# Modulation matmuls with 32 columns a quadrant, one copy out of the bank, and the first weights loaded ahead of x

## The chip, the cores and the metric

The kernel runs on one core of a Trainium2 chip. The metric is device time in microseconds (us) of one execution, as the median of several runs. The engines are named TensorE (PE in the rows; its weight loads are PEld), VectorE (DVE), ScalarE (ACT), GpSimd (POOL) and SyncE (SP), the last of which issues most of the DMA transfers.

## The reference, cut to what matters

Two layers of a hybrid backbone, fp32 throughout, for 128 context tokens and 1024 latent tokens of 1024 features. Every layer scales and shifts its normalised input by a modulation that is computed from a condition vector:

```
def ada_modulate(x, cond, norm_g, w_ada, b_ada):
    m = jax.nn.silu(cond) @ w_ada + b_ada
    shift, scale, gate = jnp.split(m, 3, axis=-1)
    h = rms_norm(x, norm_g) * (1.0 + scale[:, None, :]) + shift[:, None, :]
    return h, gate[:, None, :]
```

There are two condition vectors, `c` for the latent tokens and `c_ctx` for the context tokens, so this product has two rows; `w_ada` is 1024 x 3072 for each layer. Layer 0 then projects h by `w_in_0`, runs a convolution module and an attention side by side, and projects out; layer 1 does the same with a pooling mixer. In both, `x + gate * out` is returned.

## The kernel before, in words

Tokens go in 9 tiles of 128 (tile 8 is the context), three tiles to a group g of 384 columns. Features are cut into 8 chunks k of 128. A product in fp32 precision is made of three fp32r matmuls, of high and low parts: `split` casts a weight to its high part on ScalarE (L186) and subtracts it on VectorE for the low part (L187).

The modulation product puts the two condition vectors, after silu, as the stationary operand. `sc` (L144) holds 8 chunks x 2 columns; a matmul loads the 2 columns of a chunk and streams a strip of `w_ada`. Four strips run side by side, one in each column group of the array (`tile_position=(0, r)`, r = 0, 32, 64, 96), and so fill rows r and r + 1 of a PSUM bank. The program's fp32 matmuls appear in the trace as two records each.

Shift and scale of layer 0 come in four rounds m. `load_wada(m)` (L288) issues four strips of 512 KB on SP and, from round 1 on, one small vector behind each (`late`); `ada0_rows(m)` (L319) has the 32 matmuls and copies the four row pairs out to `ads` by four VectorE copies (L333); `ada0_cols(m)` (L335) turns them by one transpose (L338) and adds bias and norm gain into `SH` and `SC` (L273, L278, L279), two chunks k a round. All that layer 1 needs, and the gates, comes later in three strip sets, `ada_strips` (L350), 8 steps of four matmuls each, given out as background work by `ada_steps`; `ada_cols` (L379) clears a tile on GpSimd (L383) and copies four row pairs (L385), and `ada_turn` transposes it.

The start: SP issues four small vectors (one of them on ScalarE's queue), x0 to x2, the strips of round 0, the first halves of two weights (`raw0`), x3 to x5, rounds 1 and 2, the second halves, round 3, x6 and x7. `norm_x` squares a tile on ScalarE (L126), makes the reciprocal root on GpSimd (L113, L114) and scales on VectorE (L128). `h_chunk` (L441) transposes a chunk of three x tiles (L445), applies SC and SH on ScalarE (L450) and splits the result (L451, L452). `first_chains` (L470) writes by hand, under `manual_schedule`, the order of TensorE, ScalarE and VectorE: round m, then its h chunks, and the chain matmuls (L230) that they allow. `split_w0(0, 0)`, the split of the first half weight, stands ahead of that block in the program. Elsewhere a planner orders each engine's instructions by a simulated timeline. Behind `first_chains` come the rest of the projections with the convolution as background work on VectorE, ScalarE and GpSimd, the attention, the output product and layer 1.

Of the kernel before, what the change touches and what calls it, by code (L numbers as in the profile page):

```python
# [10 lines left out]
F32 = mybir.dt.float32  # L11
F32R = mybir.dt.float32r
AF = mybir.ActivationFunctionType
ALU = mybir.AluOpType
AX = mybir.AxisListType
P = 128
EPS = 1e-6
NEG = -1e30
D = 1024
# [27 lines left out]
def _body(tc, nc, A, O, const, wp, arena, tmpp, smp, psp):  # L47
# [7 lines left out]
    def slot(i, dtype=F32, name="s"):  # L55
        return arena.tile([P, SLOT], dtype, tag=f"S{i}", bufs=1, name=nm(name))
# [22 lines left out]

    ident = const.tile([P, P], F32, name="ident")  # L80
    make_identity(nc, ident)
    mhalf = const.tile([P, 16], F32, name="mhalf")
    gp.memset(mhalf, -0.5)
    corr = {}
    for w in (2, 4, 8, 16):
# [21 lines left out]
    def load_x(t):  # L107
        xt[t] = slot(XS[t], name="x")[:, :D]
        last["x"] = sy.dma_start(xt[t], x_src(t)).ins
# [9 lines left out]
    def norm_x(t):  # L119
        if t in normal:  # L120
            return
        normal.add(t)
        if t not in xt:
            load_x(t)
        ss = small(1, "ss")
        se.activation(gr[:, :D], xt[t], AF.Square, accum_out=ss)  # L126
        r = rstd_of(ss, D, 1.0 / D)
        ve.tensor_scalar(xt[t], xt[t], r, None, ALU.mult)  # L128

    last = {}  # L130
    for t in range(3):
        load_x(t)

    NV, NV0 = 102, 48
    V = const.tile([P, NV], F32, name="V")
# [5 lines left out]
    se.activation(th0, V[:, :16], AF.Tanh, scale=0.5)  # L141
    cu = small(16, "cu")
    ve.scalar_tensor_tensor(cu, th0, 1.0, V[:, :16], ALU.add, ALU.mult)
    sc = const.tile([P, 8, 2], F32, name="sc")  # L144
    ve.tensor_scalar(sc.rearrange("p k c -> p c k"), cu.rearrange("p (c k) -> p c k", c=2), 0.5, None, ALU.mult)

    vq = const.tile([P, 12], F32, name="vq")
    qn8, lgh, lbh = vq[:, 0:1], vq[:, 1:5], vq[:, 5:9]
# [3 lines left out]
    rows2, cwn = tmp("rows2"), tmp("cwn")  # L152
    knb = const.tile([P, 64], F32, name="knb")

    late = [
        (rows2[r0 - NV0 : r0 - NV0 + n, :P], src.rearrange("(r p) -> r p", p=P))
        for r0, src, n in (
            (V_CB, A["conv_b_0"], 4), (V_NG[1], A["norm_g_1"], 8), (V_BA[1], A["b_ada_1"], 24),
# [119 lines left out]
        ve.tensor_tensor(dst[:, k0 : k0 + n, :], src, b, ALU.add)  # L278
        ve.scalar_tensor_tensor(dst[:, k0 : k0 + n, :], dst[:, k0 : k0 + n, :], 1.0, g, ALU.add, ALU.mult)  # L279


    WAS = (0, 1, 4, 5, 2, 3, 6, 7, 8, 9, 10, 11, 16, 21, 22, 23)
    ads = [const.tile([P, P], F32, name=f"ads{i}") for i in range(2)]
    for t in ads:
        gp.memset(t, 0.0)
    for t in range(3):
        norm_x(t)
    first_w, wt = {}, {}  # L288

    def load_wada(m):  # L290
        for kh in range(2):
            for x in range(2):
                t = slot(WAS[4 * m + 2 * kh + x], name="wada")[:, :D].rearrange("p (k c) -> p k c", c=256)
                c0 = x * D + m * 256
                sy.dma_start(t, A["w_ada_0"][kh * 512 : (kh + 1) * 512, c0 : c0 + 256].rearrange("(k p) c -> p k c", p=P))
                wt[m, kh, x] = t
                if m and late:
                    sy.dma_start(*late.pop(0))

    raw0 = {}  # L300

    def split_w0(c, u):
        first_w[c, u] = split(*raw0[c, u])

    load_wada(0)
    raw0[0, 0] = load_raw0(0, 0)
    raw0[1, 0] = load_raw0(1, 0)
    for t in range(3, 6):
# [5 lines left out]
    load_wada(3)  # L314
    for t in (6, 7):
        load_x(t)
    split_w0(0, 0)
    adb = {}

    def ada0_rows(m):  # L320

        b = adb[m] = bank("tp")
        for k in range(8):
            for x in range(2):
                for q in range(2):
                    r = 32 * (2 * x + q)
                    te.matmul(
                        b[r : r + 2, :P], sc[:, k, :], wt[m, k // 4, x][:, k % 4, q * P : (q + 1) * P],
                        start=(k == 0), stop=(k == 7), tile_position=(0, r),
                    )  # L330
        t = ads[m % 2]
        for r in range(0, P, 32):
            ve.tensor_copy(t[r : r + 2, :], b[r : r + 2, :P])  # L333

    def ada0_cols(m):  # L335

        adt = adb[m][:, P : 2 * P]
        te.transpose(out=adt[:, :98], in_=ads[m % 2][:98, :], identity=ident[:98, :98])  # L338
        av = adt.rearrange("p (x q c) -> p x q c", x=2, q=2)
        fin_shift(0, SH[0], av[:, 0, :, 0:2], 2 * m, 2)  # L340
        fin_scale(0, SC[0], av[:, 1, :, 0:2], 2 * m, 2)
# [6 lines left out]
    def ada_strips(l, col, n, fin):  # L348

        st = {}  # L350

        def step(k):
            w = slot(ADS[st_i[0] % len(ADS)], name="wad")[:, : 4 * n]
            st_i[0] += 1
            dma_later(w, A[f"w_ada_{l}"][k * P : (k + 1) * P, col : col + 4 * n])
            if k == 0:
                st["b"] = bank("tp")
            for q in range(4):
                r = 32 * q
                te.matmul(  # L360
                    st["b"][r : r + 2, :n], sc[:, k, :], w[:, q * n : (q + 1) * n],
                    start=(k == 0), stop=(k == 7), tile_position=(0, r),
                )
            if k == 7:
                st["then"] = fin(st["b"])


        then, owed_turn[:] = list(owed_turn), [lambda: st["then"] and st["then"]()]
        adq.append(then + [lambda k=k: step(k) for k in range(4)])
        adq.append([lambda k=k: step(k) for k in range(4, 8)])  # L370
# [8 lines left out]
    def ada_cols(l, b, c0):  # L379

        t = slot(ADS[st_i[0] % len(ADS)], name="adr")[:, :G]
        st_i[0] += 1
        gp.memset(t[:98, :], 0.0)  # L383
        for r in range(0, P, 32):
            ve.tensor_copy(t[r : r + 2, :], b[r : r + 2, :G])  # L385
        return lambda: ada_turn(l, t, c0)

    def ada_turn(l, t, c0):
# [78 lines left out]
    def first_chains():  # L467


        bs = {(0, 0): (bank("mm"), bank("mm")), (1, 0): (bank("mm"), bank("mm")), (0, 1): (bank("cv"), bank("cv"))}  # L470

        def C(k, which=((0, 0), (1, 0), (0, 1))):
            for x, g in which:
                w = [first_w[x, 0], first_w.get((x, 1))]
                for i in range(2):
                    chain_ws(bs[x, g][i][:, :G], w, i * P, h0, g, ks=(k,))

        def T(k, g):
            h_chunk(g, [xt[t] for t in range(3 * g, 3 * g + 3)], 0, h0, k, "tp")

        h0[0] = hslots(range(4))
        ada0_rows(0)
        ada0_cols(0)
        T(0, 0)
        T(1, 0)
        for k in range(2):
            C(k, ((0, 0),))
        split_w0(1, 0)
        for t in range(3, 6):
            norm_x(t)  # L490
        h0[1] = hslots(range(4, 8))
        for k in range(2):
            C(k, ((1, 0),))
        T(0, 1)
        T(1, 1)
        ada0_rows(1)
        for k in range(2):
            C(k, ((0, 1),))
        ada0_cols(1)
        for k in (2, 3):  # L500
            for g in range(2):
                T(k, g)
        for m in (2, 3):
            ada0_rows(m)
            C(2 * m - 2)
            ada0_cols(m)
            T(2 * m, 0)
            T(2 * m, 1)
            if m == 2:
                split_w0(0, 1)  # L510
            C(2 * m - 1, ((0, 0), (1, 0)))
            T(2 * m + 1, 0)
            T(2 * m + 1, 1)
            if m == 2:
                split_w0(1, 1)
            C(2 * m - 1, ((0, 1),))
        for x in bs:
            for k in (6, 7):
                C(k, (x,))
        return bs  # L520
# [959 lines left out]
```

## Time and profile before

| | us |
|---|---|
| median of 3 runs (967.46 to 968.0) | 967.62 |
| the profiled execution | 967.13 |
| its span | 965.4 |
| TensorE matmul busy | 940.7 (97%) |
| VectorE busy | 602.5 (62%) |
| ScalarE busy | 403.8 (42%) |
| GpSimd busy | 368.7 (38%) |

Times in the rows below are microseconds from the span's start unless marked ns. A line of the timeline gives start, duration, engine, source line, operation, output and inputs, and in brackets the idle time of the engine ahead of it with what ended it; instructions of one kind in a row are merged (x4). A q behind an engine's name is its sequencer, which issues DMAs. The duration of a matmul holds its way through the array, so the pace of a stream is read from a merged piece in the chain of waits, divided by its count.

### The profile page before, as it was taken

The page shows a single profiled execution, that of the slowest core. Times are in us where ns is not written, and L with a number is a line of the kernel's source. Part 1 is how long each engine was busy: PE and PEld are TensorE (multiplying, and loading weights), DVE is VectorE, ACT ScalarE, POOL GpSimd, SP SyncE. Part 2 cuts the span into 40 slices and gives each one's busy share as a digit, 9 for nine tenths or more (in the row PEclk, how much of TensorE's full clock was granted, in tenths as well). Part 3 has the DMA queues.
Part 4 walks back from the last instruction along what each step waited for, and adds up shares of the span by engine and source line. Part 5 has one row for each costly group of instructions (what it writes and reads, how often), then busy time and mean ns, then how long its engine had stood idle before and what let it go on. Part 6 is the DMA issues. An engine that isn't in the chain of part 4 may idle for free.

```text
span 965.4 us, 16658 instructions
## 1 busy us (share of the span) xinstructions
PE 940.7 (97%) x6388; PEld 863.5 (89%) x6388; DVE 602.5 (62%) x1243; ACT 403.8 (42%) x815; POOL 368.7 (38%) x485
## 2 busy tenths in 40 slices
PE   4899999999999999999999999999999999999998
PEld 2799999899999999987777888899999999998887
DVE  3659999999683444457778547656335455585332
ACT  4365667675611344248886323353222222231010
POOL 2354879999944201124456246430000000004331
PEclk9999999999999999999999999999999999999999
DMA  9956955426111111135344413241110011133311
GB/s 310 301 202 142 352 197 185 154 67 230 48 47 48 47 45 44 43 100 144 116 122 149 151 44 119 98 145 44 55 41 30 30 44 55 66 117 124 109 66 66
DMA packets 87531, 108.53 MB, mean 112 GB/s; under 512 B 10701, under 2 KB 73037, under 8 KB 87340
## 3 DMA queue, kind: packets, MB, share of 16 engines
q1 hardware_dynamic: 82539, 95.93, 31.2%
q0 software_dynamic: 2576, 9.18, 2.4%
q10 hardware_dynamic: 2336, 2.36, 0.7%
q8 instruction: 50, 0.82, 0.4%
q14 instruction: 30, 0.24, 0.1%
HBM read 94.64 MB, written 21.57 MB: 120 GB/s over the span
## 4 chain that ended last, share of the span: by engine, by line
PE 81%; POOL 8%; DMA 5%; ACT 2%; DVE 2%; issue 1%; SPq 1%; DVEq 0%; ACTq 0%; POOLq 0%
PE mm L230 38%; PE mm L1216 10%; PE mm L1209 10%; PE mm L237 8%; POOL zc L555 7%; PE cv L987 3%; DMA wada<-in_w_ada 3%; PE tp L978 2%; PE mm L954 2%; PE mm L1379 2%; PE tp L445 1%; DMA raw<-in_w_in 1%; DMA raw<-in_w_out 1%; PE tp L360 1%; DMA wad<-in_w_ada 1%
## 5 line engine op out<-in xcount | busy, mean ns | idle before, releaser
L230 PE MATMUL mm<-h,whi 128*128 128x384 f32 x1504 | 388.0, 338 | 1.0 <-POOL h L452 0.4
L230 PEld LDWEIGHTS mm<-h,whi 128*128 128x128 f32 x1504 | 271.3, 188 | 4.4 <-issue 1.7
L230 PE MATMUL mm<-h,wlo 128*128 128x384 f32 x752 | 252.4, 336 | 0.0
L555 POOL TENSOR_TENSOR zc<-zc,gr 128x384 f32<-128x384 f32 x138 | 148.8, 1079 | 31.2 <-ACT gr L553 22.8
L237 PE MATMUL mm<-whi,h 128*128 128x256 f32 x864 | 156.8, 284 | 0.6 <-DVE qk L731 0.6
L230 PEld LDWEIGHTS mm<-h,wlo 128*128 128x128 f32 x752 | 141.6, 188 | 0.0
L237 PEld LDWEIGHTS mm<-whi,h 128*128 128x128 f32 x864 | 135.1, 192 | 2.7 <-issue 0.7
L237 PE MATMUL mm<-wlo,h 128*128 128x256 f32 x432 | 122.3, 283 | 0.0
L187 DVE TENSOR_TENSOR wlo<-raw,whi 128x1024 fp32r<-128x1024 f32 (+1 forms) x56 | 68.2, 1219 | 46.8 <-ACT whi L186 46.5
L566 DVE SCALAR_TENSOR_TENSOR cv<-u,convw,cv 128x384 f32<-128x384 f32 (+2 forms) x208 | 94.8, 511 | 0.8
L1216 PE MATMUL mm<-wrh,zs 128*128 128x512 f32 x288 | 92.3, 392 | 0.4 <-POOL wrh L1183 0.4
L1209 PE MATMUL mm<-whi,zs 128*128 128x512 f32 (+1 forms) x304 | 92.5, 379 | 0.0
L186 ACT CAST whi<-raw 128x1024 fp32r<-128x1024 f32 (+1 forms) x56 | 56.9, 1018 | 64.4 <-PE mm L230 25.4
L237 PEld LDWEIGHTS mm<-wlo,h 128*128 128x128 f32 x432 | 82.9, 192 | 0.0
L1223 POOL TENSOR_TENSOR y<-y,og 128x512 f32<-128x512 f32 x34 | 48.6, 1430 | 83.2 <-DVE og L1221 80.1
L553 ACT ACTIVATE gr<-u,convw 128x384 f32<-128x384 f32 (+2 forms) x128 | 64.5, 531 | 29.5 <-POOL zc L555 29.0
L972 POOL TENSOR_SCALAR p<-p,st 128x512 f32<-128x512 f32 x64 | 47.9, 760 | 46.5 <-DVE st L970 30.6
L1209 PEld LDWEIGHTS mm<-whi,zs 128*128 128x128 f32 x304 | 56.0, 188 | 10.6 <-ACT whi L186 0.2
L1216 PEld LDWEIGHTS mm<-wrh,zs 128*128 128x128 f32 x288 | 53.9, 188 | 12.0 <-POOL wrh L1183 0.8
L1221 DVE TENSOR_TENSOR og<-mm,gr 128x512 f32<-128x512 f32 x34 | 23.3, 687 | 59.3 <-PE mm L1216 34.3
L535 ACT ACTIVATE th<-mm 128x384 f32<-128x384 f32 x48 | 23.5, 489 | 81.7 <-PE mm L230 81.6
L1209 PE MATMUL mm<-wlo,zs 128*128 128x512 f32 (+1 forms) x152 | 57.2, 378 | 0.0
(215 smaller groups left out, 1393.3 us busy)
## 6 DMA issues: line engine op xcount, KB each, us to landing
raw<-in_w_in SPq DMA_DIRECT2D x28, 512.0 KB
wad<-in_w_ada SPq DMA_DIRECT2D x16, 768.0 KB
wada<-in_w_ada SPq DMA_DIRECT2D x16, 512.0 KB
raw<-in_w_in SPq DMA_DIRECT2D x32, 256.0 KB
raw<-in_w_out SPq DMA_DIRECT2D x16, 512.0 KB
y0scr<-y POOLq DMA_DIRECT2D x9, 512.0 KB, 3.1
y<-y0scr SPq DMA_DIRECT2D x9, 512.0 KB
x<-in_x_sample SPq DMA_DIRECT2D x8, 512.0 KB
```

The lines of the kernel that those rows point to most:

```text
L186: se.copy(hi[:, :n], raw[:, :n])
L187: ve.tensor_tensor(lo[:, :n], raw[:, :n], f(hi[:, :n]), ALU.subtract)
L230: te.matmul(out, wsl(units, a, k, c0, P), hsl(hs, b, k, g), start=(k == 0 and i == 0), stop=(k == nk - 1 and i == 2))
L237: te.matmul(out, hsl(hs, p, k, g, a, P), wsl(units, q, k, 0, 256), start=(k == 0 and i == 0), stop=(k == 7 and i == 2))
L553: se.activation(pr[:, o : o + n], src, AF.Copy, scale=w)
L555: gp.tensor_tensor(z, z, pr, ALU.add)
L566: ve.scalar_tensor_tensor(zp if k == 30 else acc, src, convw[:, c, k : k + 1], zp if k == NPTS[c] else acc, ALU.mult, ALU.add)
L972: gp.tensor_scalar(ps[i][:, e, :], ps[i][:, e, :], st[:, 4 + e : 5 + e], 0.0, ALU.mult, ALU.add)
L987: te.matmul(ob[64 * e : 64 * e + 64, i * P : (i + 1) * P], vw[j0 + i][x][:, 64 * e : 64 * e + 64], pts[i][:, e, n * P : (n + 1) * P], star ...
L1209: te.matmul(b[:, c0 : c0 + n], zs[p][:, k, :], WL[k // 2][q][:, k % 2, c0 : c0 + n], start=(k == 0 and i == 0), stop=(k == 7 and i == 2))
L1216: te.matmul(b, zs[p][:, k, :], WR[q][k // 3][:, k % 3, :], start=(k == 0 and i == 0), stop=(k == 7 and i == 2))
L1223: gp.tensor_tensor(yv, yv, t, ALU.add)
```

## The change

`sc` gets 48 columns, of which the last 32 are zero, and each modulation matmul loads 32 columns from column 2k on, so that it fills all 32 rows of its quadrant (rows 0 and 1 are the wanted ones, the others hold sums of other chunks' vectors with this strip, which nothing reads). One VectorE copy of all 128 partitions takes the place of four copies of 2, in the four rounds and in the later strips, and the memsets of `ads` and of the later tiles go. The strips of round 0 are issued ahead of x0 to x2; the normalisation of x0 to x2 moves behind the other loads in the program; and the split of the first half weight moves into the hand-written order, behind `ada0_cols(0)`.

```
-    mhalf = const.tile([P, 16], F32, name="mhalf")
+    mhalf = const.tile([P, 8], F32, name="mhalf")
...
     last = {}
-    for t in range(3):
-        load_x(t)
...
+    wt, late = {}, []
...
+    load_wada(0)
...
-    sc = const.tile([P, 8, 2], F32, name="sc")
-    ve.tensor_scalar(sc.rearrange("p k c -> p c k"), cu.rearrange("p (c k) -> p c k", c=2), 0.5, None, ALU.mult)
+    sc = const.tile([P, 48], F32, name="sc")
+    gp.memset(sc, 0.0)
+    ve.tensor_scalar(sc[:, :16].rearrange("p (k c) -> p c k", c=2), cu.rearrange("p (c k) -> p c k", c=2), 0.5, None, ALU.mult)
...
     ads = [const.tile([P, P], F32, name=f"ads{i}") for i in range(2)]
-    for t in ads:
-        gp.memset(t, 0.0)
-    for t in range(3):
-        norm_x(t)
...
-    load_wada(0)
+    for t in range(3):
+        load_x(t)
     raw0[0, 0] = load_raw0(0, 0)
...
     for t in (6, 7):
         load_x(t)
-    split_w0(0, 0)
+    for t in range(3):
+        norm_x(t)
...
-                        b[r : r + 2, :P], sc[:, k, :], wt[m, k // 4, x][:, k % 4, q * P : (q + 1) * P],
+                        b[r : r + 32, :P], sc[:, 2 * k : 2 * k + 32], wt[m, k // 4, x][:, k % 4, q * P : (q + 1) * P],
...
-        t = ads[m % 2]
-        for r in range(0, P, 32):
-            ve.tensor_copy(t[r : r + 2, :], b[r : r + 2, :P])
+        ve.tensor_copy(ads[m % 2], b[:, :P])
...
-                    st["b"][r : r + 2, :n], sc[:, k, :], w[:, q * n : (q + 1) * n],
+                    st["b"][r : r + 32, :n], sc[:, 2 * k : 2 * k + 32], w[:, q * n : (q + 1) * n],
...
-        gp.memset(t[:98, :], 0.0)
-        for r in range(0, P, 32):
-            ve.tensor_copy(t[r : r + 2, :], b[r : r + 2, :G])
+        ve.tensor_copy(t, b[:, :G])
...
         ada0_rows(0)
         ada0_cols(0)
+        split_w0(0, 0)
         T(0, 0)
```

## Rows read from the trace of the kernel before

**Rows 1.** The page: TensorE's busy time over the span, and two lines of the span in 40 equal slices of 24.1 us, in tenths.

```profile
PE 940.7 (97%) x6388; PEld 863.5 (89%) x6388; DVE 602.5 (62%) x1243; ACT 403.8 (42%) x815; POOL 368.7 (38%) x485
...
PE   4899999999999999999999999999999999999998
...
DMA  9956955426111111135344413241110011133311
```

**Rows 2.** Busy time of each engine by stage (the first three rows are of one table over the whole span, its first and last stage and its sum; the last is of a finer table of the start). Columns: stage, its length, busy time and count of PE, PEld, DVE, ACT, POOL, granted clock of TensorE, DMA share, GB/s.

```profile
0.00:50.00 50.00, 33.51 (x375) 26.68 (x376) 26.69 (x56) 19.76 (x30) 15.86 (x61) 1.00 0.98 303
...
870.00:965.40 95.40, 91.67 (x428) 76.69 (x426) 34.75 (x42) 9.87 (x17) 30.12 (x27) 1.00 0.25 88
sum 965.40, PE 940.75 PEld 863.46 DVE 602.46 ACT 403.81 POOL 368.70; mean PE 49.51 PEld 45.45 DVE 31.71 ACT 21.25 POOL 19.41
...
20.00:25.00 5.00, 4.29 (x15) 3.89 (x16) 3.60 (x5) 4.84 (x8) 3.04 (x5) 1.00 1.08 357
```

**Rows 3.** The chain of waits at the start, its three longest transfers: from issue, for so long.

```profile
18.25 8.04 DMA wada<-in_w_ada
...
26.31 7.50 DMA wada<-in_w_ada
...
37.49 10.17 DMA wada<-in_w_ada
```

**Rows 4.** The timeline around the fourth round: its last matmuls, its row copies, the transpose behind them.

```profile
47.71 1.04 PE L327 MATMUL tp<-wada,sc 128*2 128x128 f32 x28 [0.65 <-DMA wada<-in_w_ada]
...
48.84 1.18 DVE L333 COPY ads<-tp 2x128 f32<-2x128 f32 x4
...
51.93 0.25 PE L338 MATMUL tp<-ident,ads 98*128 98x98 f32 x1
```

**Rows 5.** The transfer view of the first 60 us: what the DMA engines moved in each 1.5 us.

```profile
GB/s 0 27 251 399 395 381 356 350 342 298 291 365 412 390 354 347 348 351 350 349 345 339 304 292 308 229 201 321 371 307 194 223 215 285 295 44 5 41 344 426
```

**Rows 6.** SP's queue: the first two issues of large transfers (timeline), and what it waited for up to 38.1 us (the longest and the shortest in total of the five waits for transfers: us in total, times, longest).

```profile
1.88 1.30 SPq L109 DMA_DIRECT2D x<-in_x_sample  x3
...
3.23 2.99 SPq L295 DMA_DIRECT2D wada<-in_w_ada  x4
...
SPq L295 <- DMA wada<-in_w_ada: 4.5, 4, 1.8
...
SPq L298 <- DMA raw<-in_w_in: 0.5, 1, 0.5
```

**Rows 7.** The timeline of the start: square and scaling of x2, the last quarter of round 0, the cast of the first half weight, the row copies, the low part, and the first chain matmul; then the same pair of matmuls at two times.

```profile
8.27 1.06 ACT L126 ACTIVATE gr<-x 128x1024 f32<-128x1024 f32 x1
...
10.61 0.76 DVE L128 TENSOR_SCALAR x<-x,rstd 128x1024 f32<-128x1024 f32 x1 [0.71 <-POOL rstd L114]
...
14.29 1.87 PE L327 MATMUL tp<-wada,sc 128*2 128x128 f32 x28 [0.95 <-DMA wada<-in_w_ada]
...
16.12 1.04 ACT L186 CAST whi<-raw 128x1024 fp32r<-128x1024 f32 x1 [6.71 <-DMA raw<-in_w_in]
16.21 1.19 DVE L333 COPY ads<-tp 2x128 f32<-2x128 f32 x4 [4.84 <-PE tp L327]
...
17.43 1.22 DVE L187 TENSOR_TENSOR wlo<-raw,whi 128x1024 fp32r<-128x1024 f32 x1
...
20.32 0.69 PE L230 MATMUL mm<-h,whi 128*128 128x384 f32 x1 [0.39 <-DVE h L451]
...
22.21 0.84 PE L230 MATMUL mm<-h,whi 128*128 128x384 f32 x2
...
24.09 0.51 PE L230 MATMUL mm<-h,whi 128*128 128x384 f32 x2
```

**Rows 8.** Single lines of the program: the row copies of the rounds and of the later strips, the memset that goes (duration in ns as min/median/max, first and last start), and one other copy out of PSUM (timeline).

```profile
L333 DVE COPY ads<-tp x16: 271/286/297, 16.2 to 49.7; 2x128 f32<-2x128 f32 x16
...
L385 DVE COPY adr<-tp x8: 539/553/567, 160.0 to 198.0; 2x384 f32<-2x384 f32 x8
...
L383 POOL MEMSET adr<- x2: 425/425/425, 139.1 to 179.4; 98x384 f32 x2
...
3.53 0.21 DVE L138 COPY V<-tp 128x48 f32<-128x48 f32 x1 [3.53 <-PE tp L137]
```

**Rows 9.** TensorE's wait behind 75 us that comes from VectorE (timeline), and two pieces of the chain of waits that leads to it.

```profile
236.54 0.36 PE L237 MATMUL mm<-whi,h 128*128 128x256 f32 x1 [0.57 <-DVE qk L731]
...
156.15 1.04 ACT whi L186
...
179.37 0.42 POOL adr L383
```

**Rows 10.** Paces: round 1 (timeline), one step group of the later strips with 256 and one with 384 columns streamed and the attention's value matmuls (chain of waits), and the weight loads of the last two kinds (by line: count, busy us, mean ns).

```profile
28.85 1.93 PE L327 MATMUL tp<-wada,sc 128*2 128x128 f32 x64 [0.43 <-ACT h L450]
...
92.13 1.84 PE tp L360 x32
...
129.51 2.74 PE tp L360 x32
...
436.24 1.90 PE cv L987 x32
...
L987 PEld LDWEIGHTS cv<-pt,vw 128*64 128x64 f32 x384 | 20.9, 137 | 3.4 <-issue 2.3 <-ACT pt L1143 0.9 <-DVE pt L1144 0.2
...
L360 PEld LDWEIGHTS tp<-wad,sc 128*2 128x2 f32 x192 | 4.4, 84 | 7.8 <-issue 5.8 <-PE mm L230 0.2 <-DMA vscr<-vst 0.2
```

More of the change, by code (lines that the diff above doesn't have):

```diff
@@ L130, in _body, with load_wada @@
     last = {}
-    for t in range(3):
-        load_x(t)
+    WAS = (0, 1, 4, 5, 2, 3, 6, 7, 8, 9, 10, 11, 16, 21, 22, 23)
+    wt, late = {}, []
+    def load_wada(m):
+        for kh in range(2):
+            for x in range(2):
+                t = slot(WAS[4 * m + 2 * kh + x], name="wada")[:, :D].rearrange("p (k c) -> p k c", c=256)
+                c0 = x * D + m * 256
+                sy.dma_start(t, A["w_ada_0"][kh * 512 : (kh + 1) * 512, c0 : c0 + 256].rearrange("(k p) c -> p k c", p=P))
+                wt[m, kh, x] = t
+                if m and late:
+                    sy.dma_start(*late.pop(0))
+    load_wada(0)
     NV, NV0 = 102, 48
@@ L153, in _body @@
     knb = const.tile([P, 64], F32, name="knb")
-    late = [
+    late += [
         (rows2[r0 - NV0 : r0 - NV0 + n, :P], src.rearrange("(r p) -> r p", p=P))
@@ L279, in fin_scale @@
         ve.scalar_tensor_tensor(dst[:, k0 : k0 + n, :], dst[:, k0 : k0 + n, :], 1.0, g, ALU.add, ALU.mult)
-    WAS = (0, 1, 4, 5, 2, 3, 6, 7, 8, 9, 10, 11, 16, 21, 22, 23)
     ads = [const.tile([P, P], F32, name=f"ads{i}") for i in range(2)]
-    for t in ads:
-        gp.memset(t, 0.0)
-    for t in range(3):
-        norm_x(t)
[L288 to L298, printed above, removed]
+    first_w = {}
     raw0 = {}
```

## The prediction

> **What bounds the kernel now.** I read the page first [rows 1]: TensorE is busy for 97% of the span and only the first two and the last of the forty slices show less than nine tenths, and in the first two the DMA engines are full. The table of stages [rows 2] says it in microseconds. In the first 50 us TensorE works 33.5, so 16.5 are idle; in the remaining 915.4 us it works 907.2, so idle time there is 8.2 in all, 3.7 of it in the last stage, where the outputs leave. From 50 us on this is a kernel bound by TensorE's own stream, and an edit can change its end in two ways only: by letting that stream start earlier, or by lengthening or shortening matmuls in it.
>
> When can it start? The chain of waits at the start [rows 3] runs through SP's queue and transfers, not through compute: a modulation strip 18.25 to 26.29, the next 26.31 to 33.81, the last strip of the last round issued at 37.49 and landing at 47.66. At 47.71 TensorE takes the last 28 records of the fourth round, after a wait of 0.65 us for exactly that transfer [rows 4]. From there the chain is TensorE. So the gate of the first part is the landing at 47.66, and work ahead of it has 0.65 us to spare.
>
> Is that landing set by bandwidth or by something that the change moves? The transfer view of the first 60 us [rows 5] gives a rate in slices of 1.5 us: 251 GB/s from 3 us on, about 400 at 4.5 to 7.5, then 290 to 412 up to 37.5, 194 to 371 behind that, and never near idle before 52 us. SP's issue times [rows 6] show that ahead of the fourth round's strips the queue waits for older transfers only, never for an engine. Until 47.66 it moves x0 to x5, four rounds of strips, four half weights of 512 KB and the small vectors.
>
> **The change, part by part.**
>
> *Order of loads.* On SP the three x issues (1.30 us together) go behind the first four strip issues (2.99 us); all else keeps its place, so no other queue is passed, and the 13.6 MB ahead of the landing are the same bytes in the same shapes. I cost the move at 0 for the landing at 47.66. Not seen in this trace is how well strips of 1 KB rows do as the very first transfers; the rates at 4.5 to 7.5 (about 400, mainly x) and in 21 to 30 (about 350, mainly strips) differ by 50 GB/s, which on the 2 MB of one round is 0.7 us, and what the strips lose in front x gains behind. Bounds: 0.7 us either way, value 0.
>
> *What starts earlier in front.* In before, the last strip quarter of round 0 is taken at 14.29, when 3.5 MB are in [rows 7]. After, these 3.5 MB end with x2, so x2 lands at about 14.3. Its square takes 1.06 (to 15.35), and from a square's end to the end of the scaling by its root mean square were 2.04 us in before (9.33 to 11.37): x2 is ready at 17.4. The first weight still lands at 16.1, its high part is cast 16.12 to 17.16. Round 0's matmuls, copy and scale can now be done well before that. Then: last transpose of x2 about 0.3 (17.7), modulation 0.65 on ScalarE (18.4); meanwhile the low part of the weight, 1.22 us on VectorE, 17.4 to 18.6; then the cast of h, 0.36, and the first chain matmul at about 19.0 instead of 20.32: 1.3 us earlier. If VectorE instead takes the copy only behind the scaling of x2, the copy (0.3), transpose (0.4) and scale (0.5) stand ahead of the low part: 18.6, 19.8, 20.2, a gain of 0.1. What the move of the split itself removes is small: in before the row copies already ran ahead of the low part (16.21 against 17.43), and only shift and scale, 0.48 us of VectorE, were queued behind it.
>
> Either gain runs into the gate: TensorE would reach the fourth round 0.1 to 1.3 us earlier and wait 0.75 to 1.95 us there instead of 0.65. Worth at the end: 0. In this stretch matmuls are spaced twice as far as later (the same pair takes 0.84 us at 22.21 and 0.51 at 24.09 [rows 7]), the pace of 1.2 GHz against 2.4, although the granted clock of the stretch is printed as 1.00 [rows 2]. Should the idle time that now falls between round 0 and the first chain prolong the slow pace by some 3 us, TensorE is later by half of that, and 0.65 + 1.3 take it.
>
> *One copy for four.* A row copy of 2x128 is 0.286 us, of 2x384 0.553, one of 128x48 was 0.21 [rows 8]: time goes with the row, not the partitions, so four become one of about 0.3 or 0.55. Per round that is 0.86 us of VectorE, over four rounds 3.4. Round 0 is dealt with above. In rounds 1 to 3 the transpose behind the copy stands, in TensorE's written order, behind chain matmuls: in round 3 the copies end at 50.02 and the transpose comes at 51.93, behind 18 chain matmuls [rows 4]. That cover hides all of it; without it the 0.86 would count once, since only round 3 lies behind the gate. In the strips behind, 2 x 1.66 us of VectorE and two memsets of 0.425 us on GpSimd go, and in front, where GpSimd is idle until the first root mean square, one memset of 128x48 replaces two of 128x128. GpSimd and VectorE are nearly full until 225 us, so I looked for what that frees: TensorE's only wait there is 0.57 us at 236.54 [rows 9]. Its chain goes back through GpSimd and ScalarE, which take turns in the convolution without a gap, and the second memset stands in it at 179.37 with 0.42 us; the first, at 139, lies ahead of 156.15, where the chain passes to a weight cast on ScalarE, and I don't count it. Bounds 0 and 0.57; I take 0.4, the memset in the chain, and count nothing more for VectorE, which the chain hardly touches.
>
> *Quadrants.* The matmuls now load 32 columns instead of 2. Streams are the same, so the question is whether the longer load hides. Records of round 1 come every 1.93/64 = 30.2 ns with four column groups and 2 columns loaded; the attention's value matmuls, with two column groups and 64 columns loaded, every 1.90/32 = 59.4 ns for the same 128 streamed columns [rows 10]. Times the groups that is 121 and 119: 32 times as many loaded columns cost nothing. Loading 32 per 30 ns is the same load per time as 64 per 59. Lower bound 0, no gain being possible in a stream whose length stays. Upper bound: the load itself lasts 84 ns with 2 columns and 137 with 64 [rows 10], so 30 columns more are about 53 x 30/62 = 25.6 ns, if nothing hid them. I take 0, the attention row being the nearest in kind.
>
> The Trainium skill speaks against this part: "TensorE: Matmul & The Clock Gate", section "LDWEIGHTS (loading the stationary operand)", has a load take its columns divided by 1.2 in ns, and Part 3 ("The mechanism") lets it overlap a running matmul only in another row group, of which there is just one here. By that the 30 columns would add 25 ns to each record, which is the first rival below, 974.0 us; by the attention rows the sum stays as it is. They speak against it here.
>
> **The sum.** Gate 0, copies 0, quadrants 0, freed engines -0.4. The profiled execution took 967.13 us (965.4 of span and 1.73 around it), which gives 966.7; the median of the runs is 967.62, 0.05% above that execution, and the same 0.4 off it gives 967.2. I forecast 967.0, between the two.
>
> **The rivals.**
>
> *Loads not hidden (slower).* 28 records behind the gate and 192 of the later strips lie on TensorE's path: 220 x 25.6 ns = 5.6 us. Rounds 1 and 2 add 128 x 25.6 = 3.3 ahead of the gate, of which 0.65 + 1.3 are covered: 1.3 more. Sum 6.9 on the profiled 967.13: 974.0 us. It becomes slower by the first nanosecond per record behind the gate, and passes 0.2% of the time (1.9 us, about what a measurement of this kernel can tell from no change) at some 9 ns per record. For it: a load never seen at this width. Against it: the equal products above. Chance 0.08.
>
> *The gate opens earlier (faster).* If the last strips land earlier by as much as TensorE has won, its 1.3 and the 0.65 wait both reach the end, and the 0.57 at 236 may go too: up to 2.5 us off 967.13, 964.6. Against it: the queue never waits for an engine ahead of those strips, so nothing won in compute reaches it. Chance 0.09.
>
> *Late x holds the first chain.* If ScalarE takes the cast of the first weight (to 17.16) ahead of x2's square, x2 is ready 2.9 us later (20.3) and the first chain starts at about 21.6, 1.3 late; 0.65 are absorbed, 0.65 remain: 967.7. Chance 0.1, within 0.2%.
>
> *Another order of the rest.* Outside the hand-ordered stretches the instructions are put in order by a planner that sees the new durations. TensorE has only 8.2 us of idle time behind 50 us, so a new order can give back little and could cost a wait or two of 1 to 2 us: 965.5 to 970, chance 0.13, of which 0.05 are over the bound.
>
> *The forecast itself*, in which nothing but the memset reaches the end: chance 0.6.
>
> **How the numbers follow.** Faster by over 0.2% (below 965.7): 0.09. Slower (above 969.6): 0.08 + 0.05 = 0.13. Within: 0.78. The range takes in the landing's 0.7 either way, the 0.57 and most of the planner's order, and leaves out the loads not hidden and most of the earlier gate: 965.2 to 969.3.
>
> **What would show it.** Right: round 0 done by about 12 us, the first chain at 19 to 20.2, the wait ahead of the fourth round grown to 0.75 to 1.95 us, the last strip landing at 47 to 48.4, records of the strips still 30, 57 and 86 ns apart. Wrong: a landing moved by over 1 us (load order), records further apart (quadrants), or idle time on TensorE behind 50 us other than about 8 us (order).

## The result, and the profile after

| | before | after |
|---|---|---|
| median (20 runs each, taken together) | 967.69 us (966.49 to 969.0) | 969.22 us (967.8 to 972.27) |
| the profiled execution | 967.13 us | 968.34 us |
| its span | 965.4 us | 966.3 us |

The ratio is 1.0021, 95% interval 1.0015 to 1.0027: by it the change costs 2.0 us (1.5 to 2.6). The forecast was no change, 967.0; the time lies inside the range, at its slow end, but the cost is clear of its interval.

A small part of it lies outside the span. The time exceeds the span by 2.01 to 2.12 us in all 20 runs of after, and by 1.72 to 1.83 in the 137 runs of before beside the experiments: 0.3 us that no wait in a profile can show. By the medians it goes with the single copies, 1.84 to 2.20 us in every kernel below that has them and 1.75 to 1.81 in every other, the one with 32 columns and four copies among them. Why, these runs don't show.

The page and the stage table (columns as in [rows 2]) show where there is no room. TensorE is as full as before [rows 1], and so is VectorE: 24.1 to 25.0 of each 25 us between 100 and 225 us in before, 23.9 to 24.8 in after. First before:

```profile
100.00:125.00 25.00, 25.00 (x166) 23.65 (x165) 24.14 (x45) 16.81 (x29) 21.77 (x22) 1.00 0.98 347
125.00:150.00 25.00, 25.00 (x170) 21.89 (x173) 24.97 (x55) 16.05 (x38) 19.27 (x20) 1.00 0.38 139
150.00:175.00 25.00, 25.00 (x227) 21.62 (x220) 24.90 (x55) 16.83 (x29) 22.84 (x21) 1.00 0.72 240
175.00:200.00 25.00, 25.00 (x218) 22.91 (x218) 24.80 (x57) 18.71 (x41) 23.27 (x23) 1.00 0.36 119
200.00:225.00 25.00, 25.00 (x211) 25.00 (x210) 24.24 (x49) 16.28 (x28) 22.80 (x22) 1.00 0.37 126
```

Then after:

```profile
PE 942.9 (98%) x6388; PEld 867.1 (90%) x6388; DVE 596.5 (62%) x1225; ACT 404.1 (42%) x815; POOL 369.7 (38%) x482
```

```profile
0.00:50.00 50.00, 36.38 (x382) 30.26 (x383) 23.33 (x44) 19.73 (x30) 15.89 (x60) 1.00 1.00 310
50.00:75.00 25.00, 23.74 (x149) 22.18 (x148) 13.05 (x28) 18.15 (x37) 13.58 (x18) 1.00 0.47 166
...
100.00:125.00 25.00, 25.00 (x166) 23.82 (x165) 24.16 (x45) 16.46 (x29) 21.69 (x22) 1.00 0.99 366
125.00:150.00 25.00, 25.00 (x167) 22.25 (x169) 24.46 (x56) 17.05 (x39) 20.99 (x19) 1.00 0.37 138
150.00:175.00 25.00, 25.00 (x226) 21.80 (x219) 24.38 (x54) 17.00 (x29) 22.86 (x21) 1.00 0.69 236
175.00:200.00 25.00, 25.00 (x219) 23.09 (x218) 24.84 (x56) 18.13 (x39) 22.43 (x21) 1.00 0.37 123
200.00:225.00 25.00, 25.00 (x212) 25.00 (x211) 23.86 (x50) 16.62 (x29) 23.18 (x22) 1.00 0.36 123
```

The timeline of after, from the row copy of round 0 to the modulation at 55 us:

```profile
13.14 0.29 DVE L333 COPY ads<-tp 128x128 f32<-128x128 f32 x1 [8.73 <-PE tp L329]
...
19.93 0.69 PE L246 MATMUL mm<-h,whi 128*128 128x384 f32 x1 [0.52 <-DVE h L449]
...
28.48 1.95 PE L329 MATMUL tp<-wada,sc 128*32 128x128 f32 x64 [0.43 <-ACT h L448]
...
45.52 2.01 PE L329 MATMUL tp<-wada,sc 128*32 128x128 f32 x64
...
53.39 0.66 ACT L448 ACTIVATE h<-tp,SH,SC 128x384 f32<-128x384 f32 x1
53.95 1.05 ACT L126 ACTIVATE gr<-x 128x1024 f32<-128x1024 f32 x1
...
54.10 0.55 PE L443 MATMUL tp<-ident,x 128*128 128x128 f32 x3
...
54.99 2.03 ACT L448 ACTIVATE h<-tp,SH,SC 128x384 f32<-128x384 f32 x3
...
55.70 0.55 PE L443 MATMUL tp<-ident,x 128*128 128x128 f32 x3 [1.05 <-ACT h L448]
```

Round 3 runs in one piece at 45.52: in this execution the strip that held it in [rows 4] was there. TensorE's transposes at 54.10 come 1.0 us earlier than in before (55.11), and all of that goes in a new wait of 1.05 us at 55.70: ScalarE has taken the square of x7 (53.95) between two modulations (53.39 and 54.99). In before the order was the other way round:

```profile
54.40 1.21 ACT L450 ACTIVATE h<-tp,SH,SC 128x384 f32<-128x384 f32 x2
...
55.11 1.11 PE L445 MATMUL tp<-ident,x 128*128 128x128 f32 x6
...
55.51 1.05 ACT L126 ACTIVATE gr<-x 128x1024 f32<-128x1024 f32 x1
```

Behind that, three more waits of TensorE differ: for VectorE's `qk` at 236.45 (0.29 us, [rows 9] had 0.57) and, new, at 263.17 (0.58), and for VectorE's `pp` at 518.54 (1.32, was 0.96). At the last matmul TensorE is 0.9 us late. A second profiled execution of the same kernel, 970.31 us long, shows what varies (waits of TensorE from 50 us on, in total, times, longest):

```profile
PE tp L443 <- ACT h L448: 2.0, 3, 1.1
PE tp L1034 <- DVE pp L1029: 1.4, 1, 1.4
PE tp L890 <- ACT pt L1136: 1.3, 1, 1.3
PE mm L253 <- DVE qk L730: 1.2, 2, 0.7
PE mm L1215 <- POOL wrh L1182: 1.0, 1, 1.0
```

### The profile page after: what moved, and what is told of

It is laid out like the page before. It is cut to its first block, busy times and chain, and to the rows that moved or that the text cites. A ratio compares the mean times of both kernels' runs of the same rounds, so it can differ in the third digit from the quotient of the medians.

```text
span 966.3 us, 16623 instructions
## 1 busy us (share of the span) xinstructions
PE 942.9 (98%) x6388; PEld 867.1 (90%) x6388; DVE 596.5 (62%) x1225; ACT 404.1 (42%) x815; POOL 369.7 (38%) x482
## 4 chain that ended last, share of the span: by engine, by line
PE 79%; POOL 10%; ACT 3%; issue 2%; DVE 2%; DMA 2%; SPq 0%; DVEq 0%; ACTq 0%; POOLq 0%
PE mm L246 39%; PE mm L1215 10%; PE mm L1208 10%; POOL zc L554 8%; PE mm L253 5%; PE cv L986 3%; PE tp L977 2%; PE mm L953 2%; PE mm L1378 2%; DMA x<-in_x_sample 2%; PE tp L443 1%; PE cv L246 1%; DMA raw<-in_w_out 1%; ACT gr L552 1%; POOL rstd L114 1%
```

## The experiments

Eighteen experiments were run, one of them the changed kernel once more, each timed against the kernel before on its own chip. Three edits are used again and again and called edges here. **S** puts the normalisation of x6 to x8, which begins with their squares, behind the last modulation on ScalarE:

```
-            se.activation(t[:, a:e], b[:, a:e], AF.Identity, bias=o, scale=s)
+            last["h"] = se.activation(t[:, a:e], b[:, a:e], AF.Identity, bias=o, scale=s).ins
...
-            norm_x(t)
+            with tc.issue_after(last["h"]):
+                norm_x(t)
```

**T** puts the eight `texp` transfers (3 MB) behind the last modulation strip on SP:

```
         for m in range(8):
-            sy.dma_start(
+            with tc.issue_after(last["d"].ins):
+                sy.dma_start(
```

**G** moves seven small operations on the gate rows, 6.6 us in after, from VectorE to ScalarE (the expectations below say eight and 7 us):

```
-            ve.tensor_scalar(r[p, a:n], r[p, a:n], 0.5, None, ALU.mult)
+            se.activation(r[p, a:n], r[p, a:n], AF.Copy, scale=0.5)
```

All results (differences between kernels of different chips are taken from the ratios, not from the medians), with TensorE's waits in each profiled execution (us; a dot where under 0.15) at the six places that matter: the last strip of round 3 (47 us), ScalarE's modulation (54 to 57), a strip of the first later set (111 to 113), VectorE's `qk` (232 to 264), `pp` or ScalarE's `p` (517), GpSimd's `wrh` (867).

| kernel | median | ratio, 95% | 47 | 55 | 112 | qk | pp | wrh |
|---|---|---|---|---|---|---|---|---|
| before | 967.69 | 1 | 0.65 | . | . | 0.57 | 0.96 | 0.41 |
| after | 969.22 | 1.0015 to 1.0027 | . | 1.05 | . | 0.87 | 1.32 | 0.20 |
| after, again | 970.28 | 1.0016 to 1.0036 | 0.74 | 1.27 | . | 1.24 | 1.36 | 1.00 |
| quadrants and copies only | 969.75 | 1.0012 to 1.0029 | . | 1.29 | 0.79 | 0.27 | 1.36 | 0.20 |
| quadrant loads alone | 970.53 | 1.0023 to 1.005 | . | 1.35 | . | 2.17 | 1.32 | 0.41 |
| load order only | 968.85 | 1.0001 to 1.0018 | . | . | 0.57 | 0.85 | 1.32 | 1.11 |
| after + S | 971.01 | 1.002 to 1.0039 | 0.50 | . | 0.49 | 2.14 | 1.31 | . |
| before + S | 966.40 | 0.9978 to 0.9995 | . | . | 0.15 | 0.59 | 0.96 | 0.27 |
| after + T | 973.98 | 1.0049 to 1.0075 | 0.58 | 1.29 | . | 3.48 | 1.32 | . |
| before + T | 967.92 | 0.999 to 1.0008 | . | 0.46 | . | 1.76 | 1.28 | 0.20 |
| after + S, T | 969.32 | 1.0014 to 1.0032 | 0.34 | . | . | 1.19 | 1.32 | 1.16 |
| before + S, T | 968.45 | 0.9999 to 1.0016 | . | . | . | 1.94 | 1.07 | . |
| after + G | 969.28 | 1.0008 to 1.0026 | 1.11 | 1.20 | 0.34 | . | 1.02 | 0.67 |
| after + S, G | 968.10 | 0.9991 to 1.0009 | 0.51 | . | 0.99 | . | 1.03 | 0.81 |
| before + S, G | 966.41 | 0.9973 to 0.999 | . | . | 0.96 | . | 1.18 | 0.15 |
| after + T, G | 968.94 | 1.0005 to 1.0022 | . | 1.33 | . | 1.13 | 1.35 | 0.18 |
| after + S, T, G | 967.19 | 0.9987 to 1.0004 | . | . | . | . | 1.38 | 1.02 |
| before + S, T, G | 965.07 | 0.9962 to 0.9983 | . | . | . | . | 1.25 | 0.31 |
| load order + S, T, G | 965.99 | 0.9973 to 0.9991 | 0.50 | . | . | . | 1.24 | 0.52 |
| quadrants, copies + S, T, G | 966.37 | 0.9978 to 0.9996 | . | . | . | . | 1.08 | 0.65 |

**The two halves of the change.** The first kernel takes from the diff only the 32 columns, the single copies and the memsets; the second only the moved loads, normalisation and split.

> The kernel before with the 32-column quadrants and the single copies alone; loads, normalisation and the first split keep their old order. Theory A (the loss comes from the order of loads at the start, through ScalarE's squares of x6 and x7, and from the new order that the planner made of the rest): the last strip is again what TensorE waits for, near 47.7 us, the strips' records stay 0.6 ns slower than with 2 columns (30.5, 58 and 86 ns apart), time within 0.5 us of before unless the planner reorders the stretch from 190 to 265 us. Rival B (the longer weight loads or the copies carry the loss): 1.5 to 2 us slower than before, as the whole change.

> The whole change without the 32-column quadrants: two columns are loaded, four copies and the memsets come back; strips of round 0 ahead of x, and the split behind the scale, stay. Theory A: TensorE passes the fourth round without waiting for a strip, at about 46 us, and waits instead near 55.7 us for ScalarE's squares of x6 or x7; time 1 to 2 us over before. Rival B: equal to before within 0.5 us.

Measured 969.75 and 968.85: both cost, the quadrant half more, the load order barely clear of no change. My theory A missed on both sides: the quadrant half cost what its rival said, and the wait at 55 us, which I expected with the new order of loads, comes with the quadrant half alone.

**Quadrant loads alone**: in before, only the two matmul lines, the size and layout of `sc` with its one memset, and the size of `mhalf` change; the four copies and the other memsets are left.

```
-                        b[r : r + 2, :P], sc[:, k, :], wt[m, k // 4, x][:, k % 4, q * P : (q + 1) * P],
+                        b[r : r + 32, :P], sc[:, 2 * k : 2 * k + 32], wt[m, k // 4, x][:, k % 4, q * P : (q + 1) * P],
```

> The kernel before with 32 loaded columns in the modulation's matmuls and nothing else: four copies of two rows, both memsets and the order of the loads stay. Theory 'the price of a matmul in the planner's eyes turns the order': the strips' records are 0.5 ns further apart (58.1 against 57.5 ns), some 0.2 us in all, but ScalarE takes the square of x7 ahead of the second modulation at 55 us, so a wait of 1.05 us for ScalarE appears there, and the time is 969 to 970 us, as with quadrants and single copies together (969.75). Rival 'the copies' part turned it': 967.7 to 968.2 us.

Measured 970.53, at least as much as with the single copies. So the cost needs neither the copies nor the loads' own time (below): the order has turned. With the 32 columns in these matmuls, ScalarE takes the square of x7 (54.54) ahead of the second modulation. (What the planner counts for such a matmul is not shown; that its order turns with them is.) The wait of 1.05 us stands in the trace of every kernel here with 32 columns and without S, and in no other. Rows of this kernel's timeline:

```profile
53.98 0.65 ACT L451 ACTIVATE h<-tp,SH,SC 128x384 f32<-128x384 f32 x1
54.54 1.04 ACT L126 ACTIVATE gr<-x 128x1024 f32<-128x1024 f32 x1
...
55.58 1.22 ACT L451 ACTIVATE h<-tp,SH,SC 128x384 f32<-128x384 f32 x2
...
56.29 0.55 PE L446 MATMUL tp<-ident,x 128*128 128x128 f32 x3 [1.05 <-ACT h L451]
...
238.94 0.36 PE L238 MATMUL mm<-whi,h 128*128 128x256 f32 x1 [2.17 <-DVE qk L732]
```

**S on both kernels.**

> The whole change, and the squares of x6, x7 and x8 on ScalarE are ordered behind the last modulation of the hand-ordered block, so that none of them stands ahead of what TensorE needs there. Theory A: the wait of 1.05 us at 55.7 us goes, TensorE is about 1 us earlier than the whole change from there to 75 us, time 1 us under the whole change, with less spread from run to run. Rival C (something else, as the landing of x6 itself or VectorE, holds TensorE next): the wait comes back in front of the transposes of x6 to x8, near 64 us, and the time is that of the whole change.

> The control: the kernel before with the same ordering of the squares of x6 to x8. Theory A: in before the landing of the last strip at 47.7 us holds TensorE and the squares are only just in time, so the time stays within 0.5 us of before. Rival: the squares held before too, and it gains about 1 us.

Measured 971.01 and 966.40. The wait at 55 us went in after, and TensorE was 1.5 us ahead of before at 56 us; yet the kernel became slower. It lost 0.49 us to a strip at 111 us, 2.14 us to `qk` at 237.43 and about 1.5 us to a slow pace behind that (last section). My theory that the squares hold the loss fell: they hold the first wait of several. The kernel before gained 1.3 us from the same edge, as the rival there had it.

**T on both, then S and T.** In before and after SP waits 1.4 and 1.7 us for the `tbias` writes before it issues `texp` at 94 to 95 us, and the strips that TensorE needs at 112 us stand behind.

> The changed kernel with one ordering edge: the eight texp transfers (3 MB, on SP's queue at 95 to 101 us, where SP waits for the tbias writes before them) go behind the last modulation strip (issued at about 171 us). Theory 'many gates with tenths to spare': part of the loss of the median run is a wait of 0.5 to 0.9 us for a strip at 111 to 113 us that some executions show (those of quadrants alone, of the load order alone and of the squares behind) and others (the profiled one of the changed kernel) don't; so no wait for a strip between 90 and 125 us, 0.4 to 1.0 us less than the changed kernel's median (968.2 to 968.8 us against 969.2), and a narrower spread of its runs than 967.8 to 972.3. Rival 'the loss is the order of ScalarE, VectorE and GpSimd behind 225 us': same as the changed kernel within 0.4 us, since the waits at 236 to 263 us for VectorE's qk take back whatever TensorE wins at 112.

> The kernel before with the same edge for texp. Its profiled execution showed no wait for a strip at 111 us. Theory 'gates': within 0.5 us of the kernel before (967.2 to 968.2 us), if anything lower, and TensorE's start times at 125 us unchanged within 0.3 us. Rival 'any edge that moves the planner's order moves the time by 1 to 2 us either way': 966 or 970 us, with new waits for VectorE, GpSimd or ScalarE between 225 and 530 us.

> The changed kernel with texp late and the squares of x6 to x8 behind the modulation on ScalarE. With the squares alone TensorE was 1.5 us ahead of the kernel before at 54 to 63 us, lost 0.5 us to a strip at 111 us and 2.1 us to VectorE's qk at 237 us. Theory 'gates': TensorE is 1.2 to 1.6 us ahead of the kernel before from 55 to 234 us, and what is left of it at the end is decided by the wait at 237 us: 966.5 to 968 us if that wait stays under 1 us, 969 to 970 us if it is 2 us again. Rival 'loss in the first 60 us': 966.5 us, since the waits there and at 111 us are all gone.

> The kernel before with both edges. With the squares alone it was at 966.40 us (ratio 0.9987), TensorE 1.4 us ahead at 54 us and 1.7 us at 235 us, of which 0.6 went at 241 us to VectorE's qk. Theory 'gates': 0 to 0.3 us less than that (966.1 to 966.4 us), since the wait for a strip at 111 us was only 0.15 us there. Rival 'any edge moves the order': 965 or 968.5 us, by new waits behind 225 us.

The wait at 112 us is in none of the four, but what that was worth has either sign: by the ratios T took 0.6 us from after + S (within the intervals), nothing from before, and added 2.0 to before + S and 4.0 to after, the slowest kernel of the study, 973.98, which neither my theory nor its rival had. Its timeline says why (VectorE's subtractions for the low parts and its first reduction, GpSimd's step behind it, TensorE), and the table of 5 us stages what came on top (columns as in [rows 2]):

```profile
222.66 2.04 DVE L203 TENSOR_TENSOR wlo<-raw,whi 128x1024 fp32r<-128x1024 f32 x1
...
225.80 1.97 DVE L203 TENSOR_TENSOR wlo<-raw,whi 128x1024 fp32r<-128x1024 f32 x1
...
230.04 0.68 DVE L724 TENSOR_REDUCE ssq<-sq 128x8 f32<-128x512 f32 x1
...
230.81 0.20 POOL L113 TENSOR_SCALAR rstd<-ssq 128x8 f32<-128x8 f32 x1 [4.12 <-DVE ssq L724]
...
240.81 0.36 PE L253 MATMUL mm<-whi,h 128*128 128x256 f32 x1 [3.02 <-DVE qk L730]
```

```profile
240.00:245.00 5.00, 4.20 (x22) 4.23 (x23) 2.85 (x6) 2.70 (x6) 4.76 (x6) 0.66 0.00 0
```

In after the same reduction starts at 225.65 and GpSimd takes its result at once:

```profile
225.65 0.68 DVE L724 TENSOR_REDUCE ssq<-sq 128x8 f32<-128x512 f32 x1
...
226.42 0.20 POOL L113 TENSOR_SCALAR rstd<-ssq 128x8 f32<-128x8 f32 x1
...
236.45 0.36 PE L253 MATMUL mm<-whi,h 128*128 128x256 f32 x1 [0.29 <-DVE qk L730]
```

Between 222 and 230 us VectorE has no gap: the reduction stands in its queue behind convolution taps and two subtractions. So my next theory was that VectorE's queue, nearly full from 100 us on, is the second bound of the first 265 us.

**G, on four kernels**, tests it: 6.6 us of work taken off VectorE.

> The changed kernel with the eight halvings of the gate rows (2x256 and 2x384, 0.5 to 1.1 us each, at 119 to 123 and 203 to 208 us) moved from VectorE to ScalarE: about 7 us less on VectorE, which is busy for 24.2 to 25.0 of each 25 us from 100 to 225 us, and some 3 us more on ScalarE, which is busy for 16 to 18 of 25. Theory 'VectorE's queue is the second bound up to 265 us': the waits for VectorE's qk at 236 and 263 us (0.3 and 0.6 us in the changed kernel's profile) go, TensorE is 0.5 to 1.0 us ahead of the changed kernel at 270 us, and the time is 968.0 to 968.8 us against 969.2. Rival 'GpSimd's convolution sets it': no change at 236 and 263 us, 969.0 to 969.5 us. Rival 'any edit redeals the order': 967 or 971 us by a wait elsewhere.

> The changed kernel with the squares of x6 to x8 behind the modulation, and the gate rows' halvings on ScalarE. Without the second edit TensorE was 1.2 us ahead of the kernel before at 63 us, 0.8 at 111 us, then waited 2.1 us for VectorE's qk at 237 us with 1.4 us more lost at a halved pace behind it, and ended at 971.0 us. Theory 'VectorE's queue': about 7 us less of VectorE's work ahead of 237 us takes away that wait and the slow pace, so 3 to 3.5 us less: 967.3 to 968 us. Rival 'GpSimd's convolution': the wait at 237 us stays over 1.5 us, and the time at 970.5 to 971.5 us.

> The kernel before with the same two edits. With the squares behind alone it ran in 966.40 us, with a wait of 0.6 us for VectorE's qk at 241 us. Theory 'VectorE's queue': that wait goes, 965.6 to 966.2 us. Rival 'GpSimd's convolution': 966.2 to 966.6 us, the wait unchanged.

> The changed kernel with texp behind the last strip, which ran in 974.0 us because VectorE reduced the first ssq at 230.0 instead of 225.7 us, GpSimd waited 4.1 us for it and TensorE 3.0 us for qk at 241 us (and 1.2 us more at a halved pace), and with the gate rows' halvings on ScalarE. Theory 'VectorE's queue': 7 us less on VectorE ahead of that reduction bring it back to about 226 us, and 4.3 of the 4.8 us come back: 969 to 970 us. Rival 'late weights': the reduction waited for work that came late by transfers behind texp on SP's queue, not by VectorE's own load; then 973 to 974 us stay.

Measured 969.28, 968.10, 966.41 and 968.94. By the ratios after + T came back by 4.6 us, after + S by 2.8, the reduction at 226.67 and 223.60 us. With G, `qk` holds TensorE in one of eight executions (1.13 us, at 243.47, in after + T, G), without it in all twelve (0.27 to 3.48). S and T change the order too, and in none of the kernels with them and without G did that wait go. This theory stands for the waits. For the time, after + S, G and after + T, G came out within 0.1 us of what it gave; for after + G alone the time moved by less than its interval and lies in the range of the rival on GpSimd, so my expectation missed: the waits at 236 and 263 us went as expected, but this execution had 0.34 us at 112 us and 0.67 at 867. For before + S, G there is no gain over S either, and the time is in its rival's range, though the wait for `qk` went: `qk` gave 0.59 and a strip at 111.90 us took 0.96.

**All three edges.**

> The changed kernel with all three reliefs: squares of x6 to x8 behind the modulation, texp behind the last strip, the gate rows' halvings on ScalarE. Theory 'three gates that the new order met': no wait over 0.7 us for ScalarE, VectorE or a strip between 50 and 500 us, TensorE 0.7 to 1.3 us ahead of the kernel before from 56 to 500 us, 966.4 to 967.3 us. Rival 'the change itself costs': 968 us or more, against 966.4 us or less for the kernel before with the same three.

> The kernel before with the same three. Without texp late it ran in 966.41 us with 1.0 us of wait for a strip at 112 us. Theory 'gates': that wait goes and 0.5 to 1.0 us of it reach the end, 965.4 to 966 us. Rival 'what is won ahead is waited for at VectorE's queue': 966.2 to 966.8 us.

> The changed kernel once more, unchanged, for a second profiled execution and a second median. Theory 'gates that vary': the median is 1.3 to 2.0 us above the kernel before's again, and this profiled execution differs from the first by tenths at the strip of 46.5 us, at ScalarE's modulation at 55 us and at the strip of 112 us (up to 0.9 us there, none in the first). Rival 'fixed order': TensorE's start times equal those of the first execution within 0.2 us throughout, with 0.9 us above the kernel before at the end.

After once more came to 970.28, 2.6 us above before on its chip, where I expected 1.3 to 2.0. After + S, T, G gave 967.19, level with before; before + S, T, G gave 965.07, ratio 0.9973 (0.9962 to 0.9983), faster than both kernels. Neither has a wait at the first four places. Their waits behind 500 us, after's first:

```profile
PE tp L1036 <- DVE pp L1031: 1.4, 1, 1.4
...
PE mm L1217 <- POOL wrh L1184: 1.0, 1, 1.0
```

```profile
PE tp L1037 <- DVE pp L1032: 1.2, 1, 1.2
...
PE mm L1218 <- POOL wrh L1185: 0.3, 1, 0.3
```

From 40 to 515 us every matmul starts within 0.2 us of its twin in the other, but the last starts 1.2 us later with the change, 0.7 of it at `wrh`, whose cast waits for a weight from HBM. The three edges make both kernels faster by much the same, so what the change costs is the same with them, 2.1 us between the medians of one chip, as without, 2.0. The waits that they remove are therefore not shown to be what it costs: they are what can be won from the order in either kernel. In the two profiled executions, 1.9 us apart, 1.2 are there at the last matmul, 0.3 come between it and the end of the span, and 0.4 lie outside the span. So I split once more.

> The kernel before with the three reliefs and the change's order of loads (strips ahead of x, the first split later), without quadrants or single copies. Theory 'the rest comes from the 32 columns and the order that they turn': 965.0 to 965.8 us, as without the load order (965.07). Rival 'the load order costs': 966.5 to 967.3 us.

> The kernel before with the three reliefs, quadrants and single copies, and the old order of loads. Theory 'the rest comes from the 32 columns and the order that they turn': 966.5 to 967.3 us, near the changed kernel with the three (967.19). Rival 'a landing at 865 us that varies': a median between 965 and 966 us, with single runs up to 967.

965.99 and 966.37, each between its theory and its rival: by the ratios the load order keeps 0.9 us and the quadrant half 1.4, with intervals that overlap that of before + S, T, G, and neither alone holds the rest. In their profiles TensorE ends 0.4 and 0.7 us behind before + S, T, G, with `wrh` waits of 0.52 and 0.65 against 0.31. That wait follows the length of one transfer; in before + S, T, G and after + S, T, G (issue, length):

```profile
856.62 7.05 DMA raw<-in_w_out
```

```profile
857.12 7.81 DMA raw<-in_w_out
```

In the two executions of after it took 6.98 and 7.79 us. The wait is over 0.7 us in five of the eleven executions with the new order of loads and in none of the nine with the old; whether the change makes that transfer longer or it only varies, these runs don't settle.

## Why the prediction was wrong

*What it read rightly.* The row copy took 0.29 us ([rows 8] gave about 0.3). Round 0 was copied at 13.4 us (12 said), the first chain matmul came at 19.93 (19.0 to 20.2). In the second execution the wait for the strip was 0.74 us, at the edge of the 0.75 to 1.95 that were said; in the first there was none, since the landing itself lay at least about a microsecond earlier than in [rows 3]. I had bounded it with 0.7 either way from transfer rates. Over these kernels the wait is 0 to 1.1 us, and it shows in seven of eleven executions with the new order of loads and in one of nine with the old. So the early start does often run into that landing, as the prediction had it, but the 0.65 us that I read as the gate of before was the luck of one execution: the other eight, of edited kernels with the old order, have no such wait.

*Quadrants.* The value 0 was right on TensorE: 32 records take 1.93 us in the timeline for 1.91 with two columns, the wider strips 2.79 for 2.76 (both at 92 and 129 us), round 1 1.95 for 1.93 [rows 10]. That is 0.3 to 0.9 ns a record, at most 0.4 us for all 448, so the rival of loads not hidden fell. The rule of the Trainium skill that the prediction weighed ("TensorE: Matmul & The Clock Gate", "LDWEIGHTS (loading the stationary operand)") would add 25 ns to each; the trace disagrees. What is seen of the edit's price on TensorE comes by the order, first at ScalarE.

*The step that failed* is the reading of room: "idle time there is 8.2 in all ... an edit can change its end in two ways only", and with it "count nothing more for VectorE, which the chain hardly touches". By the rows of after that idle time grew from 8.2 to 9.8 us (916.3 us of span behind 50 us, 906.5 of them busy), the prediction's own sign for order. TensorE's little idle time showed what was waited for in one execution, not how near other queues stood. At 55 us ScalarE, at 112 us a strip, and up to 263 us VectorE follow TensorE within some tenths. VectorE's 24 to 25 of each 25 us between 100 and 225 us were there to read; I used them for the memset on GpSimd only and booked 0.4 us of gain. That wait went from 0.57 to 0.29 in one execution and was 0.67 in the next, and another of 0.58 came at 263 us. A second term was put at nothing without a reason: the 1.73 us around the span, taken over as it stood, became 2.0 to 2.1. Which of the new waits make up the rest of the 2.0 us stays open: with the waits at 55 us, at 112 us and for `qk` gone from both kernels, the difference between them was still 2.1.

*The rival that came nearest* is "another order of the rest": the new order and the waits that it brings are in the traces, and the time lies in its 965.5 to 970. That the order makes all of the cost is not shown, and the 0.3 us outside the span are not in it. Its chance was put at 0.13. It could have been sized: at every place where TensorE's wait is a few tenths, ask what stands ahead in the releaser's in-order queue and what one swap costs. At 55 us that is one square, 1.05 us.

*Gains don't add where queues follow each other.* S won 1.5 us at 56 us and lost it at 237; T took away the wait at 112 and lost more at 241; together with G, which alone won nothing clear of noise in after, they made 2.4 us on after and 2.6 on before.

## What to carry to other kernels

When one engine is at 97%, read the others' busy share stage by stage before pricing an edit at zero. Here VectorE, nearly full for 125 us in a row, was a second bound, and work that stood in its queue in another order came out as a wait of TensorE. Where a planner orders the queues, an edit of one kind of matmul can be an edit of the order on other engines; look at the list ahead of each near wait, and pin it, in both kernels, before judging the edit itself. And profile the same kernel twice: here two executions of one file ended 2.0 us apart, with other waits, and a wait of before that looked like a gate was in one of nine executions with the old order of loads.

## What the runs showed of the hardware

VectorE's subtraction of two SBUF operands, 128x1024, takes 1.21 us or up to 2.04 us, by what GpSimd does beside it (timeline of after below). In after it started first, at 220.08, and GpSimd's addition of 128x384, 1.01 us elsewhere, took 2.02; in after + T one of GpSimd's additions had begun 0.26 us ahead, and the subtraction at 222.66 took 2.04.

```profile
218.72 1.01 POOL L554 TENSOR_TENSOR zc<-zc,gr 128x384 f32<-128x384 f32 x1
...
220.08 1.21 DVE L203 TENSOR_TENSOR wlo<-raw,whi 128x1024 fp32r<-128x1024 f32 x1
...
220.14 2.02 POOL L554 TENSOR_TENSOR zc<-zc,gr 128x384 f32<-128x384 f32 x1 [0.41 <-ACT gr L552]
```

The Trainium skill, "SBUF — State Buffer", section "SBUF: two separate sides", says that the two engines share one pair of ports as an exclusive lock for a whole instruction; these rows agree. Here it makes the order of two queues a matter of up to 0.8 us each time.

After an idle stretch TensorE fell to little over half its pace in two of the three kernels looked at here. In after + S, behind the wait of 2.14 us, it ran a microsecond at the old pace, then pairs of records that had come every 0.36 us came every 0.64 from 238.5 to 241.6 us, and the granted clock was 0.85 and 0.81 in the two stretches of 5 us; 17 records took 3.5 us instead of 2.0. In after + T, behind 3.02 us, the granted clock was 0.66, with the same loss of 1.5 us. Behind 2.17 us in the kernel with quadrant loads alone it stayed at 1.00. First after + S, then that kernel:

```profile
238.10 0.40 PE L253 MATMUL mm<-whi,h 128*128 128x256 f32 x2
...
238.46 0.59 PE L253 MATMUL mm<-whi,h 128*128 128x256 f32 x2
...
239.07 0.63 PE L253 MATMUL mm<-whi,h 128*128 128x256 f32 x2
...
239.71 0.63 PE L253 MATMUL mm<-whi,h 128*128 128x256 f32 x2
```

```profile
235.00:240.00 5.00, 2.86 (x19) 2.68 (x18) 2.38 (x6) 2.46 (x6) 4.76 (x6) 0.85 0.00 0
240.00:245.00 5.00, 5.00 (x37) 5.00 (x37) 4.82 (x9) 3.70 (x9) 4.76 (x5) 0.81 0.00 2
```

```profile
240.00:245.00 5.00, 5.00 (x44) 5.00 (x43) 3.45 (x7) 3.02 (x8) 4.76 (x6) 1.00 0.00 0
```
